# Down projection, first half: one matmul of 512 columns where there were two of 256

## The chip, the cores and the metric

The kernel runs on one core of one Trainium2 chip. The metric is the device time of one execution in microseconds, as a median of several runs. Beside the timed runs stands one profiled execution with its trace; all rows below come from that execution. Engines: PE is TensorE's matmul (PEld its weight load), DVE VectorE, ACT ScalarE, POOL GpSimd, SP the queue that issues the DMAs.

## The reference

One layer of a diffusion backbone runs over 128 context and 2048 latent tokens (2176 tokens in all, 1024 wide). What matters here is its last part, the feed-forward block and the final norm:

```python
h2 = rmsnorm(x, norm2) * (1 + scale2) + shift2
up = conv3(h2 @ w_up)                 # 1024 -> 2 * 2816, three taps
a, gg = jnp.split(up, 2, axis=-1)
x = x + gate2 * ((jax.nn.silu(gg) * a) @ w_down)   # 2816 -> 1024
y = rmsnorm(x, final_norm)
```

All data are float32. The mLSTM scans, the short convolution and the output projection before it are not touched.

## The kernel before

Features lie on the 128 partitions and tokens on the free axis, so that a matmul has a 128x128 block of a weight matrix as its stationary operand and a row of tokens as its moving one. To keep float32 precision each operand is split into a rounded high part and a remainder (`wh`, `wl` and `th`, `tl`), and each product is three matmuls: high by high, high by low, low by high.

The up and the down projection are both computed by a seven-product block scheme. Tokens are cut in two halves `hf` of `HN = (1024, 1152)`, each of two blocks `blk` (512 or 576 tokens). The down projection is 14 products `w` (`PRODS`, seven for each half). A product has four units `mp`, one for each pair of output rows. A unit runs over the 11 tiles of the contraction in three steps (`KS = (4, 4, 3)`), so there are 12 steps in a product. In a step, for each piece `p` of the unit's tokens, each tile issues the three matmuls of lines 1201 to 1203 into that piece's own PSUM bank, `acc[p]`. Before the change a unit's block of tokens is two pieces of a quarter of the half: 256 columns in the first half, 288 in the second. The banks come in the turn `abcabca` from a pool of seven (three named `pa`, two `pb`, two `pc`); an eighth, `st`, serves the norms.

Around the matmuls:

- Weights. `stages` loads one 704 KB block a unit into `st` (line 328, two buffers), and `part` makes `wh` on ACT (line 278) and `wl` on DVE (line 279), a step at a time, two steps ahead of the matmuls (three buffers each). The load of the next unit waits until DVE is done with the buffer.
- Tokens. `Chunk` loads one of three parts of the next product's moving operand (`F<-uD`, line 1042, two buffers) and splits it into `tH` and `tL` (lines 1048 and 1049) in a ring of six.
- Results. After a unit's last step `close` (line 1068) adds its bank, times the gate, to each of the one to four output blocks that this product belongs to (`DOWN`), on DVE: one instruction for a piece, two for the piece in which context ends and latent tokens begin. The seven products of a half have 14 such blocks, times four units.
- Norms. When a block of tokens is complete, its squares are summed (lines 1078 and 1079). `norm` then makes the reciprocal root, in `inv_rms` (PE column sums, line 128; DVE, line 131; POOL, line 132) and `spread` (PE, line 139), scales the eight output tiles (line 1091), stores them (`out_y<-o`, line 1095) and loads the second half's residual into the same buffers (`o<-xD`, line 1060). It is a generator, `fin`, and is advanced by one piece a step, or by two in the second half's products 0 and 5. In the first half it runs once for each of the two pieces: the first piece only scales, the second scales, stores and loads.

SP carries all of these transfers in one queue. Within a queue instructions run in the order that was set when the kernel was built. Independent work may stand there in another order than in the code, as the rows below show it.

Of the kernel before, what the change touches and what calls it, by code (L numbers as in the profile page):

```python
# [35 lines left out]
HN = (1024, 1152)  # L36
# [15 lines left out]
def spans(t0, t1):  # L52

    return [(a, b, v) for a, b, v in ((t0, min(t1, P), 0), (max(t0, P), t1, 1)) if a < b]
# [3 lines left out]
def hymba_kernel(ctx: ExitStack, tc: tile.TileContext, I, O):  # L58
    nc = tc.nc
    V, S, G, PE, Q = nc.vector, nc.scalar, nc.gpsimd, nc.tensor, nc.sync  # L60
# [61 lines left out]
    def inv_rms(ss, n, r):  # L122

        nch = (n + P - 1) // P
        ps = pst.tile([P, 512], F32, name="st")
        for i in range(nch):
            w = min(P, n - i * P)
            PE.matmul(ps[:w, i:i + 1], ss[:, i * P:i * P + w], ones[:, 0:1], start=True, stop=True)
        for i0, i1, w in ((0, n // P, P), (n // P, nch, n % P)):
            if i0 < i1 and w:  # L130
                V.tensor_scalar(r[:w, i0:i1], ps[:w, i0:i1], 1.0 / D, EPS, op0=ALU.mult, op1=ALU.add)
                G.tensor_tensor(r[:w, i0:i1], r[:w, i0:i1], mhalf[:w, i0:i1], op=ALU.pow)

    def spread(r, n):

        ps = pst.tile([P, 512], F32, name="st")
        for i in range((n + P - 1) // P):
            w = min(P, n - i * P)
            PE.matmul(ps[:, i * P:i * P + w], bc(r[:w, i:i + 1], [w, P]), ident[:w, :w], start=True, stop=True)
        return ps  # L140
# [14 lines left out]
    def squares(b, xt):  # L155
        n = BL[b][1]
        ss = ssp.tile([P, 384], F32, name="ss")
        for k in range(KT):
            x = xt[k // 4][:, k % 4, :n]
            if k == 0:  # L160
                S.activation(ss[:, :n], x, AF.Square)
                continue
            sq = sqp.tile([P, 384], F32, name="sq")
            S.activation(sq[:, :n], x, AF.Square)
            V.tensor_add(ss[:, :n], ss[:, :n], sq[:, :n])
        return ss
# [27 lines left out]
    def make_h(b, src, norm):  # L194
        return apply(b, load_x(b, src, xp, "xt", 2), norm)
# [122 lines left out]
                k: (lambda mp, i=i: wD[mp, i]) for i, k in enumerate(("s1", "s2", "s4", "s3"))}}  # L318
    PRODS = [(hf, x) for hf in range(2) for x in range(7)]

    def units_of(w):
        if w == 13:
            return [(mp, (p,)) for p in range(2) for mp in range(4)]
        return [(mp, (0, 1)) for mp in range(4)]
# [643 lines left out]
    with ph2:  # L968
# [5 lines left out]
        def bank(kind):  # L974
            return pu.tile([P, 512], F32, name="p" + kind, bufs=3 if kind == "a" else 2)
# [77 lines left out]
        outs, sst = {}, {}  # L1053

        def load_out(hf, m, blk):
            n = HN[hf] // 2
            t0 = hf * HN[0] + blk * n
            t = (op if blk else dp).tile([P, 576], F32, name=f"o{m}")
            outs[m, blk] = t[:, :n]
            Q.dma_start(outs[m, blk], xD[m][:, t0:t0 + n])  # L1060

        def close(hf, m, blk, p, acc):
            n = HN[hf] // 4
            t0 = hf * HN[0] + (2 * blk + p) * n
            q = outs[m, blk][:, p * n:(p + 1) * n]
            for a, e, v in spans(t0, t0 + n):
                a, e = a - t0, e - t0
                V.scalar_tensor_tensor(q[:, a:e], acc[:, a:e], modT[:, 40 + m, v:v + 1], q[:, a:e],
                                       op0=ALU.mult, op1=ALU.add)

        def square(m, blk, a, e, first=False):
            if first:
                if a == 0:
                    sst[blk] = dp.tile([P, 576], F32, name="ss", bufs=2)
                S.activation(sst[blk][:, a:e], outs[m, blk][:, a:e], AF.Square)
                return
            sq = dp.tile([P, 576], F32, name="sq", bufs=2)
            S.activation(sq[:, a:e], outs[m, blk][:, a:e], AF.Square)
            V.tensor_add(sst[blk][:, a:e], sst[blk][:, a:e], sq[:, a:e])

        def norm(hf, blk, p, then=None):

            n = HN[hf] // 4
            t0 = hf * HN[0] + 2 * blk * n
            r = dp.tile([P, 4], F32, name="fr", bufs=2)
            inv_rms(sst[blk][:, p * n:(p + 1) * n], n, r)
            yield
            rb = spread(r, n)
            for m in range(KT):
                q = outs[m, blk][:, p * n:(p + 1) * n]  # L1090
                V.scalar_tensor_tensor(q, q, nrm[:, 2, m:m + 1], rb[:, :n], op0=ALU.mult, op1=ALU.mult)
                if hf:
                    Q.dma_start(O["y"][m][:, t0 + p * n:t0 + (p + 1) * n], q)
                elif p:
                    Q.dma_start(O["y"][m][:, t0:t0 + 2 * n], outs[m, blk])
                    then(m)
                if m % 2:
                    yield
# [4 lines left out]
                yield  # L1103

        def norms(hf, blk):
            for p in range(2):
                yield from norm(hf, blk, p, lambda m: load_out(1, m, blk))

        split(0, ORDER[2])
# [6 lines left out]
        def take():  # L1116
            w = next(prods, None)
            if w:
                ahead.append(w)
            return ahead.pop(0)  # L1120

        for hf, j, i in ((hf, j, i) for hf in range(2) for j in range(FT) for i in range(7)):
# [13 lines left out]
            for p in range(2):  # L1136
# [3 lines left out]
                for kk in range(4):  # L1140
                    rh, rl = (t[:, 4 * p + kk] for t in slots[ORDER[i]])
                    w = slice(kk * P, (kk + 1) * P)
# [7 lines left out]
                m, blk, other = {3: (0, 1, 2), 4: (1, 1, 1), 5: (0, 0, 0), 6: (1, 0, None)}[i]  # L1150
# [35 lines left out]
        fin = iter(())  # L1186
        step = 0
        for w, (hf, x) in enumerate(PRODS):
            n = HN[hf] // 4
            for mp, ps in units_of(w):  # L1190
                acc = {p: bank(next(turn))[:, :n] for p in ps}
                for c, nk in enumerate(KS):
                    while loads and loads[0][0] - 3 <= step:
                        loads.pop(0)[1].load()
                    wh, wl = take()
                    th, tl = ds[RING[w % 2][c]]
                    for p in ps:
                        for kk in range(nk):
                            k = slice(kk * P, (kk + 1) * P)
                            t = slice((2 * kk + p) * n, (2 * kk + p + 1) * n)  # L1200
                            PE.matmul(acc[p], wh[:, k], th[:, t], start=(c == kk == 0), stop=False, skip_group_check=True)  # L1201
                            PE.matmul(acc[p], wh[:, k], tl[:, t], start=False, stop=False, skip_group_check=True)  # L1202
                            PE.matmul(acc[p], wl[:, k], th[:, t], start=False, stop=(c == 2 and kk == nk - 1),  # L1203
                                      skip_group_check=True)
                    if c == 2:
                        for row, blk in DOWN[x][2]:
                            for p in ps:
                                close(hf, mp + 4 * row, blk, p, acc[p])
                    if jobs and jobs[0][0] + 1 <= step:
                        k, ch = jobs[0]  # L1210
                        ch.split(step - k - 1, 2)
                        if step == k + 2:
                            jobs.pop(0)
                    if w == 0:
                        next(cv, None)
                    if step == 9:
                        for _ in cv:
                            pass
                        phu.close()
                        dp = ph2.enter_context(tc.tile_pool(name="dp", bufs=1, side="right"))  # L1220
                        for m in range(KT):
                            load_out(0, m, 0)
                    for _ in range(2 if hf and x in (0, 5) else 1):
                        next(fin, None)
                    step += 1
                if w == 13:
                    square(mp, 0, ps[0] * n, (ps[0] + 1) * n)
                    if ps == (0,) and mp == 3:
                        fin = norm(hf, 0, 0)
            if x == 4:  # L1230
                fin = chain(squares(hf, 1, range(KT), True), norms(hf, 1))
            if x == 5:
                fin = chain(fin, squares(hf, 0, range(4, KT), True))
            if w == 6:
                fin = chain(fin, squares(hf, 0, range(4), False), norms(hf, 0))
# [68 lines left out]
```

## Time and profile before

| | |
|---|---|
| median of 3 runs | 2519.47 us (2518.98 to 2521.13) |
| profiled execution | 2520.55 us, of which the span of its instructions is 2518.8 us |
| PE busy | 98% of the span |
| DVE, ACT, POOL busy | 69%, 44%, 3% |

The span is what the trace covers; the rest of the execution's time lies around it. Matmuls overlap one another, so that the duration of one says little; what counts is the distance from the start of one to the start of the next.

### The profile page before, as it was taken

To read this page: it belongs to the slowest core of one execution; us is meant where nothing else is said; L and a number is where in the kernel's file an instruction comes from. 1 tells how busy PE (TensorE), PEld (TensorE's weight loads), DVE (VectorE), ACT (ScalarE), POOL (GpSimd) and SP (SyncE) were. 2 spreads that over 40 slices of the span, in tenths; PEclk is the share of its full clock that TensorE was granted. 3 is DMA by queue.
4 is the path that set the end of the run, shared out by engine and by line. 5 is a ranking of instruction groups with operands and counts; after the bars stand their busy time and mean duration, and the time that the engine had idled before them with its cause. 6 is when DMAs were issued, how large, how long until landed. Compare 5 with 4: busy or idle time off the path is not lost.

```text
span 2518.8 us, 46131 instructions
## 1 busy us (share of the span) xinstructions
PE 2464.3 (98%) x17967; PEld 2446.1 (97%) x17967; DVE 1740.9 (69%) x3401; ACT 1100.6 (44%) x2109; POOL 67.0 (3%) x130
## 2 busy tenths in 40 slices
PE   8999999999999989999999999999999999999998
PEld 8999999999999989999999999999999999999998
DVE  4995443343467767889798879776767787677665
ACT  4521143333344444555454446544545543443343
POOL 0000000000011110000000000000000000000000
PEclk9999999999999999999999999999999999999999
DMA  8888733466567886977456446544444485576544
GB/s 287 281 278 268 224 102 105 140 205 211 175 199 205 256 272 199 291 249 250 149 198 210 151 158 229 186 155 157 149 163 143 158 299 202 189 241 221 181 158 145
DMA packets 252445, 506.29 MB, mean 201 GB/s; under 512 B 22963, under 2 KB 153155, under 8 KB 241347
## 3 DMA queue, kind: packets, MB, share of 16 engines
q1 hardware_dynamic: 252226, 503.35, 60.5%
q8 instruction: 141, 2.31, 0.4%
q14 instruction: 78, 0.63, 0.1%
HBM read 355.24 MB, written 148.03 MB: 200 GB/s over the span
## 4 chain that ended last, share of the span: by engine, by line
PE 77%; DVE 9%; DMA 9%; issue 2%; ACT 2%; SPq 1%; POOL 0%; DVEq 0%; ACTq 0%; POOLq 0%
PE pa L1143 7%; PE pa L1145 7%; PE pa L1144 7%; PE acc L206 5%; PE acc L208 5%; PE acc L207 5%; PE pb L1145 3%; PE pb L1143 3%; PE pb L1144 3%; DVE jk L555 3%; PE pa L1203 2%; PE pa L1201 2%; PE pa L1202 2%; DMA wD<-wm 2%; DMA R<-nD 2%; PE pc L1144 2%
## 5 line engine op out<-in xcount | busy, mean ns | idle before, releaser
L206 PE MATMUL acc<-hH,wh 128*128 128x384 f32 (+1 forms) x1536 | 513.7, 334 | 5.5 <-DVE cr L425 3.0
L208 PE MATMUL acc<-hH,wl 128*128 128x384 f32 (+1 forms) x1536 | 504.9, 329 | 0.0
L207 PE MATMUL acc<-hL,wh 128*128 128x384 f32 (+1 forms) x1536 | 504.2, 328 | 0.0
L1143 PE MATMUL pa<-tH,wh 128*128 128x272 f32 x1408 | 409.2, 291 | 4.1 <-DVE row L483 2.9
L1145 PE MATMUL pa<-tH,wl 128*128 128x272 f32 x1408 | 407.9, 290 | 0.0
L1144 PE MATMUL pa<-tL,wh 128*128 128x272 f32 x1408 | 405.9, 288 | 0.0
L278 ACT ACTIVATE wh<-st 128x512 fp32r<-128x512 f32 (+1 forms) x312 | 188.7, 609 | 418.9 <-PE pa L1144 118.2
L206 PEld LDWEIGHTS acc<-hH,wh 128*128 128x128 f32 x1536 | 290.3, 189 | 7.5 <-DVE cr L425 3.4
L207 PEld LDWEIGHTS acc<-hL,wh 128*128 128x128 f32 x1536 | 290.1, 189 | 0.7
L208 PEld LDWEIGHTS acc<-hH,wl 128*128 128x128 f32 x1536 | 290.1, 189 | 0.3 <-issue 0.2
L984 DVE SCALAR_TENSOR_TENSOR tt<-raw,fw,tt 128x127 f32<-128x127 f32 (+4 forms) x264 | 242.2, 947 | 47.3 <-ACT tt L990 46.2
L279 DVE TENSOR_TENSOR wl<-st,wh 128x512 fp32r<-128x512 f32 (+1 forms) x312 | 205.4, 660 | 98.8 <-ACT wh L278 93.3
L1143 PEld LDWEIGHTS pa<-tH,wh 128*128 128x128 f32 x1408 | 265.7, 189 | 5.1 <-DVE row L483 3.1
L1144 PEld LDWEIGHTS pa<-tL,wh 128*128 128x128 f32 x1408 | 266.1, 189 | 0.0
L1145 PEld LDWEIGHTS pa<-tH,wl 128*128 128x128 f32 x1408 | 265.4, 189 | 0.0
L1143 PE MATMUL pb<-tH,wh 128*128 128x272 f32 x704 | 203.6, 289 | 0.4 <-ACT wh L278 0.4
L1145 PE MATMUL pb<-tH,wl 128*128 128x272 f32 x704 | 203.6, 289 | 0.0
L1144 PE MATMUL pb<-tL,wh 128*128 128x272 f32 x704 | 202.7, 288 | 0.0
L278 ACT ACTIVATE wh<-s 128x512 fp32r<-128x512 f32 x176 | 110.9, 630 | 148.1 <-PE pc L1144 90.5
L1203 PE MATMUL pa<-tH,wl 128*128 128x256 f32 (+1 forms) x528 | 152.6, 289 | 0.2 <-DVE wl L279 0.2
L1201 PE MATMUL pa<-tH,wh 128*128 128x256 f32 (+1 forms) x528 | 152.8, 289 | 0.0
L1202 PE MATMUL pa<-tL,wh 128*128 128x256 f32 (+1 forms) x528 | 152.4, 289 | 0.0
(236 smaller groups left out, 5485.3 us busy)
## 6 DMA issues: line engine op xcount, KB each, us to landing
st<-in_w_up SPq DMA_DIRECT2D x88, 512.0 KB, 4.5
wst<-in_w_in SPq DMA_DIRECT2D x48, 512.0 KB, 4.2
wU<-s SPq DMA_DIRECT2D x22, 1024.0 KB, 6.6
s<-wU SPq DMA_DIRECT2D x22, 1024.0 KB, 5.7
st<-wD SPq DMA_DIRECT2D x32, 704.0 KB, 4.9
st<-in_w_down SPq DMA_DIRECT2D x28, 704.0 KB, 4.1
R<-nD SPq DMA_DIRECT2D x34, 512.0 KB, 5.6
wm<-in_w_modr SPq DMA_DIRECT2D x32, 512.0 KB, 4.9
```

Source lines behind the costliest of these rows:

```text
L206: PE.matmul(acc[:, :n], w_h, hH[:, k, :n], start=(k == 0), stop=False)
L207: PE.matmul(acc[:, :n], w_h, hL[:, k, :n], start=False, stop=False)
L208: PE.matmul(acc[:, :n], w_l, hH[:, k, :n], start=False, stop=(k == KT - 1))
L278: S.activation(wh[:, :n], a, AF.Copy)
L279: V.tensor_sub(wl[:, :n], a, wh[:, :n].bitcast(F32))
L984: V.scalar_tensor_tensor(o, i, w, o, op0=ALU.mult, op1=ALU.add)
L1143: PE.matmul(acc, wh[:, w], rh, start=(kk == 0 and i in (0, 1, 5)), stop=False, skip_group_check=True)
L1144: PE.matmul(acc, wh[:, w], rl, start=False, stop=False, skip_group_check=True)
L1145: mm = PE.matmul(acc, wl[:, w], rh, start=False, stop=(kk == 3), skip_group_check=True)
L1201: PE.matmul(acc[p], wh[:, k], th[:, t], start=(c == kk == 0), stop=False, skip_group_check=True)
L1202: PE.matmul(acc[p], wh[:, k], tl[:, t], start=False, stop=False, skip_group_check=True)
L1203: PE.matmul(acc[p], wl[:, k], th[:, t], start=False, stop=(c == 2 and kk == nk - 1), skip_group_check=True)
```

## The change

In the first half of the down projection a unit has one piece of 512 columns, a whole PSUM bank, where it had two of 256. `NP` gives the number of pieces in each half. `close`, `norm` and the slices of the moving operand follow it, so that in the first half the norm of a block runs once over 512 tokens. The second half stays as it was.

```diff
+    NP = (1, 2)
+
     def units_of(w):
+        if w < 7:
+            return [(mp, (0,)) for mp in range(4)]
         if w == 13:
...
         def close(hf, m, blk, p, acc):
-            n = HN[hf] // 4
-            t0 = hf * HN[0] + (2 * blk + p) * n
+            n = HN[hf] // 2 // NP[hf]
+            t0 = hf * HN[0] + (NP[hf] * blk + p) * n
...
         def norm(hf, blk, p, then=None):
-            n = HN[hf] // 4
-            t0 = hf * HN[0] + 2 * blk * n
+            n = HN[hf] // 2 // NP[hf]
+            t0 = hf * HN[0] + NP[hf] * blk * n
...
-                elif p:
-                    Q.dma_start(O["y"][m][:, t0:t0 + 2 * n], outs[m, blk])
+                else:
+                    Q.dma_start(O["y"][m][:, t0:t0 + n], q)
                     then(m)
...
         def norms(hf, blk):
-            for p in range(2):
+            for p in range(NP[hf]):
                 yield from norm(hf, blk, p, lambda m: load_out(1, m, blk))
...
         for w, (hf, x) in enumerate(PRODS):
-            n = HN[hf] // 4
+            n = HN[hf] // 2 // NP[hf]
...
-                            t = slice((2 * kk + p) * n, (2 * kk + p + 1) * n)
+                            t = slice((NP[hf] * kk + p) * n, (NP[hf] * kk + p + 1) * n)
```

## Rows read from the trace of the kernel before

**Rows 1.** The page's first lines: span, busy time and share of each engine, instructions.

```profile
span 2518.8 us, 46131 instructions
...
PE 2464.3 (98%) x17967; PEld 2446.1 (97%) x17967; DVE 1740.9 (69%) x3401; ACT 1100.6 (44%) x2109; POOL 67.0 (3%) x130
```

**Rows 2.** Busy time by stretch, first half of the down projection, in six stretches.

```profile
core 0: us, PE busy (x) PEld busy (x) DVE busy (x) ACT busy (x) POOL busy (x), PEclk, DMA share, GB/s
2024.00:2064.00 40.00, 40.00 (x337) 40.00 (x336) 33.06 (x51) 19.10 (x28) 0.00 (x0) 1.00 0.85 316
2064.00:2104.00 40.00, 40.00 (x336) 40.00 (x336) 36.64 (x76) 17.41 (x25) 0.00 (x0) 1.00 0.68 230
...
2224.00:2247.00 23.00, 23.00 (x192) 22.80 (x191) 17.00 (x31) 9.50 (x15) 0.00 (x0) 1.00 0.94 322
sum 223.00, PE 223.00 PEld 222.80 DVE 168.68 ACT 100.64 POOL 1.96; mean PE 37.17 PEld 37.13 DVE 28.11 ACT 16.77 POOL 0.33
```

**Rows 3.** What PE waited for in the whole span: us in total, times, longest.

```profile
PE pb L1201 <- ACT wh L278: 3.2, 1, 3.2
...
PE st L139 <- POOL fr L132: 2.9, 3, 1.1
...
PE pa L1203 <- DVE wl L279: 0.2, 1, 0.2
```

**Rows 4.** Groups by line and shape, PE: the first of the three lines of matmuls.

```profile
line engine op names shapes xcount | busy us, mean ns | idle before us <-releasers
...
L1201 PE MATMUL pa<-tH,wh 128*128 128x256 f32 x264 | 74.7, 283 | 0.0
...
L1201 PE MATMUL pb<-tH,wh 128*128 128x256 f32 x176 | 50.0, 284 | 0.0
...
L1201 PE MATMUL pc<-tH,wh 128*128 128x256 f32 x176 | 49.8, 283 | 0.0
```

**Rows 5.** PE in order of time: first and last of 103 matmuls of 256 columns.

```profile
start us, us, engine line op out<-in xcount [idle before <-releaser]
2101.80 0.28 PE L1203 MATMUL pc<-tH,wl 128*128 128x256 f32 x1
...
2113.97 0.28 PE L1203 MATMUL pb<-tH,wl 128*128 128x256 f32 x1
```

**Rows 6.** The same: first and last of 101 matmuls of 288 columns.

```profile
2317.71 0.30 PE L1202 MATMUL pb<-tL,wh 128*128 128x288 f32 x1
...
2330.94 0.30 PE L1203 MATMUL pa<-tH,wl 128*128 128x288 f32 x1
```

**Rows 7.** The same, output of w_in: first and last of 47 of 384 columns.

```profile
96.17 0.34 PE L206 MATMUL acc<-hH,wh 128*128 128x384 f32 x1
...
104.14 0.33 PE L207 MATMUL acc<-hL,wh 128*128 128x384 f32 x1
```

**Rows 8.** The same, another 47 of 384 columns.

```profile
176.92 0.34 PE L206 MATMUL acc<-hH,wh 128*128 128x384 f32 x1
...
185.01 0.34 PE L207 MATMUL acc<-hL,wh 128*128 128x384 f32 x1
```

**Rows 9.** Groups by line and shape, DVE, 2024 to 2247 us.

```profile
L1068 DVE SCALAR_TENSOR_TENSOR o<-pa,modT,o 128x256 f32<-128x256 f32 x36 | 16.4, 477 | 1.3 <-PE pa L1203 1.3
...
L1091 DVE SCALAR_TENSOR_TENSOR o<-o,nrm,st 128x256 f32<-128x256 f32 x16 | 6.9, 474 | 0.0
...
L1068 DVE SCALAR_TENSOR_TENSOR o<-pa,modT,o 128x128 f32<-128x128 f32 x20 | 6.0, 342 | 3.4 <-PE pa L1203 3.4
```

**Rows 10.** In order of time, DVE and then PE: start of product 1's second unit.

```profile
2061.98 1.29 DVE L279 TENSOR_TENSOR wl<-st,wh 128x512 fp32r<-128x512 f32 x2 [1.91 <-ACT wh L278]
...
2063.11 0.28 PE L1201 MATMUL pa<-tH,wh 128*128 128x256 f32 x1
```

**Rows 11.** SP in order of time, second half's first product (time is that of issuing).

```profile
2257.53 0.32 SPq L328 DMA_DIRECT2D st<-wD  x1
2264.69 0.32 SPq L1042 DMA_DIRECT2D F<-uD  x1
2268.96 2.30 SPq L1095 DMA_DIRECT2D out_y<-o  x4
2271.60 2.68 SPq L1060 DMA_DIRECT2D o<-xD  x4
2274.33 2.27 SPq L1095 DMA_DIRECT2D out_y<-o  x4
2278.21 2.21 SPq L1060 DMA_DIRECT2D o<-xD  x4
2280.47 0.90 SPq L328 DMA_DIRECT2D st<-in_w_down  x2
```

**Rows 12.** PE in order of time, 2284.7 to 2291.4 us.

```profile
2284.76 0.29 PE L1203 MATMUL pa<-tH,wl 128*128 128x288 f32 x1
2288.24 0.61 PE L1201 MATMUL pb<-tH,wh 128*128 128x288 f32 x1 [3.19 <-ACT wh L278]
...
2291.29 0.36 PE L1202 MATMUL pb<-tL,wh 128*128 128x288 f32 x1
```

**Rows 13.** Busy time in the stretch behind that wait (columns as in rows 2).

```profile
2288.70:2291.00 2.30, 2.30 (x11) 2.30 (x11) 1.29 (x3) 0.43 (x2) 0.00 (x0) 0.50 0.57 203
```

## The prediction

> **What bounds the kernel now.** I read the page's first lines before anything else. PE is busy for 98% of the span, DVE for 69%, ACT for 44% [rows 1]. A sum over stages can mislead, so I cut the first half of the down projection into stretches. There PE is busy in all of the 223 us, at the full granted clock of 1.00 (2.4 GHz). DVE is busy for 168.68 us of them, but for 36.64 of 40 us between 2064 and 2104, and the DMA engines are 94% busy in the last 23 us [rows 2]. The list of PE's waits confirms it: in the down projection's loop it stood once, 3.2 us, for weights, three times for POOL in the norms, 2.9 us together, and 0.2 us for a remainder of weights [rows 3]; all but the last of these lie behind the 223 us. So in the changed stage the distance from one matmul to the next sets the time, and anything else counts only if it makes PE wait.
>
> **The matmuls.** The rows of line 1201 sum to 264 + 176 + 176 = 616 matmuls of 256 columns, and the three lines make 1848 of them [rows 4]. Afterwards there are 924 of 512 columns. The same columns are streamed; 924 matmuls and 924 weight loads go.
>
> What one costs is read from starts, because durations overlap. With 256 columns 103 starts span 2113.97 - 2101.80 = 12.17 us, 119.3 ns each [rows 5]. With 288 it is 13.23 us over 100 distances, 132.3 ns [rows 6]. With 384 there are two cases: 7.97 us over 46, 173.3 ns [rows 7], and 8.09 us over 46, 175.9 ns [rows 8]. A column at 2.4 GHz takes 0.417 ns, so 256 columns take 106.7 ns, 288 take 120.0 and 384 take 160.0. What is left for each matmul is 12.6, 12.3, and 13.3 to 15.9 ns. It hardly grows with the columns: it is a price for a matmul, and half of the matmuls no longer pay it.
>
> No row shows 512 columns. The kindest extrapolation takes the slope between 256 and 288 (13.0 ns over 32 columns, 0.406 ns a column): 119.3 + 256 x 0.406 = 223.3 ns. The harshest takes the slope from 288 to the slow 384 (43.6 ns over 96, 0.454): 175.9 + 128 x 0.454 = 234.0 ns. A pair of 256 costs 2 x 119.3 = 238.6 ns, so a pair gains 4.6 to 15.3 ns, and 924 pairs 4.3 to 14.1 us. Between them lie 213.3 ns of columns plus the 384's own 13.3 to 15.9, which is 226.6 to 229.2. I take 228 ns, since 384 is the nearest row: 10.6 ns a pair, **9.8 us** in all.
>
> The Trainium skill speaks against so much: its page "TensorE: Matmul & The Clock Gate", section "Wait — 56ns, not 53.3ns?", gives a warm matmul its columns at 2.4 GHz and only about 2.5 ns beside them. By that rule 924 matmuls fewer would gain an estimated 2.3 us. This case's rows don't agree for these float32 pairs of weight load and matmul: 256 columns would take 109.2 ns by the rule and take 119.3.
>
> **DVE.** A close of 256 columns is 477 ns in the mean and one of 128 columns 342 ns [rows 9], 1.05 ns a column. One of 512 is then 477 + 256 x 1.05 = 746 ns, against 954 for two. By the time in which they were busy (16.4 us for 36 and 6.0 us for 20) the pair is 911 ns and the one 767. With 14 blocks times four units there are 56 pairs, so DVE is relieved of 8 to 12 us. The piece with the context tokens stays cut at 128. The norms' scaling loses 16 of 32 instructions in the same way. This buys nothing directly, since PE doesn't wait for DVE here. It does matter that PE will ask for its weights 5% faster: DVE's 168.68 us in 223 become some 158 in 213, the same 75%.
>
> A bank of 512 columns is complete only at the unit's end, where before the first piece was complete nine matmuls (1.1 us) earlier. So the closes start that much later, and end at about the same time, being shorter. With one bank a unit instead of two, a bank is asked for again after seven units instead of three and a half, which is the cover: I cost this at nothing. Without it the price would be one close, 0.75 us, at each of 28 units.
>
> **Norm.** Column sums and spreading work on 128 tokens at a time, so PE has the same number of them. DVE's and POOL's steps run once instead of twice a block. The eight stores and eight loads of a block stay, but their order changes: they come with the first, now only, pass, five advances of `fin` earlier. That is five steps (13 us at 223 / 84 = 2.65 us a step) for the block finished in the first half, and two and a half steps for the one finished behind it, where two advances are made a step. On SP they will pass other weight and token loads than before, and this is the part that no row of before can settle.
>
> The price is in the rows. In the second half's first product, SP issued a weight load at 2257.53, a token load at 2264.69, then 16 stores and loads until 2280.4, and only then two weight loads at once [rows 11]. The first of these was late: PE stood for 3.19 us until ACT had made its `wh`, and started again at half clock, 0.50 [rows 12, 13]. From 2284.76 to 2291.29 there are 13 starts; at 132.3 ns they would have taken 1.7 us and took 6.5. So this wait cost 4.8 us. Moved to an earlier place, the 16 transfers may leave that load free (a gain of up to 4.8 us), or delay another one as much (a loss of about as much if the old wait stays too). I take 0 with both ends kept. The wait for POOL, 1.1 us at most [rows 3], stays: there the column sums and the spreading are still one advance apart.
>
> **Sum.** 2520.55 us of the profiled execution - 9.8 = 2510.7 us. That execution lies 1.1 us above the median of 2519.47, so I forecast 2519.47 - 9.8 = 2509.7 us, 0.39% less. A difference of 0.2%, 5 us, is about what a measurement can tell from none.
>
> **Rivals.**
>
> *The late weight load disappears.* The stores no longer stand ahead of the load at 2280.47. For it speaks that they move forward by more than two steps; against it, that the other loads of that product had only the same queue. Gain 9.8 + 4.8 = 14.6 us: 2504.9 us.
>
> *The supply doesn't follow.* Where DVE and DMA are busiest, weights arrive shortly before they are needed: in product 1's second unit the first of two remainders that end at 2063.27 was done at about 2062.6, and PE began at 2063.11 [rows 10], half a microsecond later. PE gains 66/2 x 10.6 = 0.35 us a unit, so by that sixth unit it would come 1.7 us earlier, and stand for about 1.2 us unless DVE's shorter closes make up for it. Together with a second delayed load of 3 to 4 us half of the gain is lost: about 2514.5 us.
>
> *The 12 to 16 ns aren't the matmul's own price*, but come with the columns (a slower stream from SBUF, say). For it speaks that the remainder is largest at 384; against it, that it is no larger at 288 than at 256. At 119.3 / 256 = 0.466 ns a column 512 take 238.6 ns, as much as the pair, and nothing is gained; but 384 would then take 178.9 ns, and even the slow case is 175.9. At 175.9 / 384 = 0.458 ns 512 take 234.5 ns and 3.8 us are gained. So 2515.7 to 2519.5 us, no change that a measurement can tell. By the rule of the Trainium skill's page named above the result would be an estimated 2517 us.
>
> *Slower*, by one mechanism: the 16 transfers, now earlier, hold up weight loads on SP in both places. Each stop costs 4.8 us, so it takes more than two such new stops to eat 9.8 us, and more than three (9.8 + 5.0 = 14.8 us) to be slower by over 0.2%. For it speaks that 94% of the DMA engines' time was taken where the first block's transfers ended [rows 2]; against it, that these now come before that stretch. Four stops would give about 2529 us.
>
> **Chances.** The forecast with small changes of the waits (2506 to 2514) 0.57; the late load gone 0.20; supply or a new wait 0.12, half of it still over 0.2% faster; no price of the matmul's own 0.07; slower 0.04. That makes faster 0.57 + 0.20 + 0.06 = 0.83, same 0.06 + 0.07 = 0.13, slower 0.04. For 8 in 10 I take 2503.5 to 2514 us: the forecast, the better case, and the nearer edge of the supply case; the bounds of a pair alone give 2505.4 to 2515.2.
>
> **What would show it.** Right: 924 matmuls of 512 columns, starts 226 to 230 ns apart, a first half of the down projection of some 213 us, closes of 512 columns near 750 ns, DVE's share unchanged. Wrong: starts above 234 ns, an idle PE behind line 278 or 279 in products 0, 1 or 6, or a stop of more than 3 us behind a weight load that SP issued after a row of stores.

## The result, and the profile after

The changed kernel takes 2506.47 us in the median of six runs (2500.30 to 2509.24), beside 2520.30 us for the kernel before on the same chip. The ratio is 0.9939 with a 95% interval of 0.9925 to 0.9952: 0.61% faster, 12 to 19 us (the medians alone differ by 13.8 us). The forecast was faster by 9.8 us, at 2509.7 us. The way was right, and so was the gain in the first half; a second gain came in the second half, where the forecast had put 0. The profiled execution took 2504.05 us.

The page's first lines, after:

```profile
span 2502.2 us, 44204 instructions
...
PE 2454.3 (98%) x17043; PEld 2398.2 (96%) x17043; DVE 1731.5 (69%) x3327; ACT 1100.3 (44%) x2109; POOL 62.9 (3%) x128
```

Against [rows 1] 924 matmuls are gone and the span is 16.6 us shorter. To see where, both traces are divided at the down projection's matmuls: at the start of the first, of the first of the second half and of the last. The kernel before has these at 2023.66, 2246.92 and 2506.51 us, the changed one at 2023.90, 2237.48 and 2490.66 us. So the first half lasts 213.6 us in place of 223.3 (9.7 less), the second half, which the change doesn't touch, 253.2 in place of 259.6 (6.4 less), and what lies behind the last start 0.7 less.

The changed matmuls, in order of time: first and last of 54 in a row, and the groups of their first line by shape.

```profile
2101.82 0.40 PE L1207 MATMUL pa<-tL,wh 128*128 128x512 f32 x1
...
2113.94 0.39 PE L1206 MATMUL pb<-tH,wh 128*128 128x512 f32 x1
```

```profile
L1206 PE MATMUL pa<-tH,wh 128*128 128x512 f32 x132 | 51.5, 390 | 0.0
L1206 PE MATMUL pc<-tH,wh 128*128 128x512 f32 x88 | 34.7, 394 | 0.1
L1206 PE MATMUL pb<-tH,wh 128*128 128x512 f32 x88 | 34.4, 390 | 0.0
```

That is 12.12 us over 53 distances, 228.7 ns, against 119.3 ns for half as many columns [rows 5]. Over the whole stage the mean distance is 228.3 ns, and before it was 119.7, if the 10 of 923 and 11 of 1847 distances are left out in which PE stopped or worked for the norms; with all of them it is 231.1 and 120.8.

Busy time by stretch in the first half (columns as in [rows 2]):

```profile
2024.00:2064.00 40.00, 40.00 (x176) 32.51 (x175) 32.85 (x43) 19.93 (x29) 0.00 (x0) 1.00 0.89 326
...
2214.00:2237.00 23.00, 22.90 (x99) 18.14 (x98) 16.32 (x25) 11.71 (x17) 0.00 (x0) 1.00 0.91 337
sum 213.00, PE 212.90 PEld 174.50 DVE 159.90 ACT 102.37 POOL 1.20; mean PE 35.48 PEld 29.08 DVE 26.65 ACT 17.06 POOL 0.20
```

PE still has no room. DVE is busy for 159.90 of 213 us, the same three quarters as in [rows 2]; weight loads no longer fill PEld.

What PE waited for from 2015 to 2500 us, all of it:

```profile
PE st L139 <- POOL fr L132: 1.9, 2, 1.1
PE st L128 <- DVE ss L1084: 1.7, 1, 1.7
```

The wait of 3.2 us for weights [rows 3] is gone, and one of the three for POOL, of 1.0 us. The wait of 1.7 us for DVE, behind the last of these matmuls, was there before with the same length. The reason why the weights are in time stands in SP's queue in the second half's first product, the answer to [rows 11]:

```profile
2247.91 0.32 SPq L333 DMA_DIRECT2D st<-wD  x1
2250.78 2.57 SPq L1100 DMA_DIRECT2D out_y<-o  x4
2255.63 2.12 SPq L1065 DMA_DIRECT2D o<-xD  x4
2257.80 2.69 SPq L1100 DMA_DIRECT2D out_y<-o  x4
2263.13 2.84 SPq L1065 DMA_DIRECT2D o<-xD  x4
2266.02 1.78 SPq L333 DMA_DIRECT2D st<-in_w_down  x2
```

The 16 transfers still stand ahead of the weight load for product 8's first unit. That load is now issued 28.5 us after the second half began (2266.02 - 2237.48), where it was 33.6 us (2280.47 - 2246.92). The next two rows show how little more than enough that is in this execution: DVE finishes the first remainder of these weights at 2273.53 + 0.69 = 2274.22, and PE begins the product at 2274.58.

```profile
2273.53 0.69 DVE L279 TENSOR_TENSOR wl<-st,wh 128x512 fp32r<-128x512 f32 x1 [1.28 <-ACT wh L278]
...
2274.58 0.29 PE L1206 MATMUL pb<-tH,wh 128*128 128x288 f32 x1
```

### The profile page after: what moved, and what is told of

The parts are those of the page before. It is cut to its first block, busy times and chain, and to the rows that moved or that the text cites. A ratio compares the mean times of both kernels' runs of the same rounds, so it can differ in the third digit from the quotient of the medians.

```text
span 2502.2 us, 44204 instructions
## 1 busy us (share of the span) xinstructions
PE 2454.3 (98%) x17043; PEld 2398.2 (96%) x17043; DVE 1731.5 (69%) x3327; ACT 1100.3 (44%) x2109; POOL 62.9 (3%) x128
## 4 chain that ended last, share of the span: by engine, by line
PE 79%; DMA 8%; DVE 8%; issue 1%; ACT 1%; SPq 1%; POOL 0%; DVEq 0%; ACTq 0%; POOLq 0%
PE pa L1148 7%; PE pa L1150 7%; PE pa L1149 7%; PE acc L206 6%; PE acc L208 6%; PE acc L207 6%; PE pb L1150 4%; PE pb L1148 3%; PE pb L1149 3%; DVE jk L560 3%; PE pa L1206 3%; PE pa L1207 3%; PE pa L1208 3%; DMA wD<-wm 2%; PE pc L1208 2%; PE pc L1206 2%
## 5 line engine op out<-in xcount | busy, mean ns | idle before, releaser
L114 DVE TENSOR_TENSOR wl<-wst,wh 128x512 fp32r<-128x512 f32 (+1 forms) x160 | 105.9, 687 | 64.2 <-ACT wh L111 64.2
L279 DVE TENSOR_TENSOR wl<-s,wh 128x512 fp32r<-128x512 f32 x176 | 120.7, 687 | 29.0 <-ACT wh L278 25.4
L1148 PEld LDWEIGHTS pb<-tH,wh 128*128 128x128 f32 x704 | 132.4, 188 | 0.6 <-ACT wh L278 0.6
```

Of the source, the lines that this page charges most:

```text
L114: V.tensor_sub(wl[:, a:a + n // 2], st[:, a:a + n // 2], wh[:, a:a + n // 2].bitcast(F32))
L279: V.tensor_sub(wl[:, :n], a, wh[:, :n].bitcast(F32))
L1148: PE.matmul(acc, wh[:, w], rh, start=(kk == 0 and i in (0, 1, 5)), stop=False, skip_group_check=True)
```

## The experiments

In the comparisons below the runs of one kernel lie up to 18 us apart, and in the profiles the down projection starts anywhere from 2017.2 to 2030.9 us, by what happens before it. So beside each ratio to the kernel before stand the two halves of the down projection from the one profile of each kernel, each from the start of its first matmul to the start of its last. For the kernel before they are 223.1 and 259.6 us, for the changed one 213.4 and 253.2.

**The matmuls alone.** Units, banks and closes as in the changed kernel, the first half's norms in two passes again.

```diff
         def norm(hf, blk, p, then=None):
-            n = HN[hf] // 2 // NP[hf]
-            t0 = hf * HN[0] + NP[hf] * blk * n
+            n = HN[hf] // 4
+            t0 = hf * HN[0] + 2 * blk * n
...
-                else:
-                    Q.dma_start(O["y"][m][:, t0:t0 + n], q)
+                elif p:
+                    Q.dma_start(O["y"][m][:, t0:t0 + 2 * n], outs[m, blk])
...
-            for p in range(NP[hf]):
+            for p in range(2):
```

> Matmuls of 512 columns, one bank and one close as in the changed kernel, but the first half's norms again in two passes of 256 tokens, stores with the second pass. Theory (two separate gains: the price of 924 matmuls, and the single pass of the norm which moves 16 stores and loads ahead of a weight load): the first half of the down projection takes 213 to 214 us, and in the second half PE stands again for 2 to 5 us at the first unit of product 8, behind a weight load that was issued after the stores. Total 9 to 11 us below the kernel before, 4 to 7 us above the changed kernel. Rival (the earlier PE alone moved the queue, the norm edit does nothing): no such stand, and the time of the changed kernel within 2 us.

Ratio 0.9960 (0.9948 to 0.9973), halves of 217.9 and 259.6 us. The starts are 228.3 ns apart, stops again left out. PE's waits from 2015 to 2500 us, the longest sums among them:

```profile
PE pa L1206 <- ACT wh L278: 2.6, 2, 2.3
PE pb L1206 <- ACT wh L278: 2.3, 1, 2.3
PE st L139 <- POOL fr L132: 1.8, 2, 0.9
```

The second half keeps its stand, and all of its old length. The total is as expected, but not the first half: it lost 4.5 of its 9.7 us to new stands and a granted clock of 0.50 behind the largest of them. That one is of 2.3 us, until 2227.66 us, and in SP's queue a weight load left at 2220.20 us behind ten of the first block's 16 transfers: 7.5 us lie between, and in [rows 11, 12] it is 7.8 us from the late load to PE's start. That is the rival in which the supply doesn't follow, and only the other part of the edit keeps it away. Without the norm's single pass the 924 matmuls fewer are worth 5.2 us in this stage, about half.

**The norm alone.** The other half of the edit: units of two times 256 columns, the first half's norms in one pass of 512 tokens. The lines are given against the changed kernel.

```diff
     def units_of(w):
-        if w < 7:
-            return [(mp, (0,)) for mp in range(4)]
...
         def close(hf, m, blk, p, acc):
-            n = HN[hf] // 2 // NP[hf]
-            t0 = hf * HN[0] + (NP[hf] * blk + p) * n
+            n = HN[hf] // 4
+            t0 = hf * HN[0] + (2 * blk + p) * n
...
-                            t = slice((NP[hf] * kk + p) * n, (NP[hf] * kk + p + 1) * n)
+                            t = slice((2 * kk + p) * n, (2 * kk + p + 1) * n)
```

> Matmuls of 256 columns in two banks and closes of 256 as before the change; only the first half's norms run in one pass of 512 tokens. Theory of two separate gains: the first half of the down projection stays at 223 us, the stand of 3.2 us at product 8 and its half clock go, 4 to 7 us below the kernel before. Rival (the queue moved only because PE was earlier): within 2 us of the kernel before, with the stand of 3 us still there.

Ratio 0.9967 (0.9956 to 0.9978), halves of 224.0 and 254.2 us. The stand is gone, as expected by the theory of two gains; the ratio says 8 us, the halves 4.5. The rival, that the earlier PE alone moved the queue, falls with both runs: with an earlier PE and the old norm the stand is there, with the old PE and the new norm it isn't. The first half, 224.0 us, gains nothing by the norm.

**One bank, two matmuls.** Bank, close and norm of the changed kernel, but 256 columns a matmul.

```diff
-                    for p in ps:
+                    for p in ((0, 1) if hf == 0 else ps):
...
+                            m = HN[hf] // 4
+                            t = slice((2 * kk + p) * m, (2 * kk + p + 1) * m)
+                            o = acc[p] if hf else acc[0][:, p * m:(p + 1) * m]
...
```

> The changed kernel with its one bank, its closes of 512 columns and its norm in one pass, but each matmul of 512 columns issued as two of 256 into the two halves of that bank, in the order of the kernel before. Theory (a price for each matmul of 12 to 13 ns): 1848 matmuls 119 to 120 ns apart, the first half of the down projection 223 us, 9 to 11 us above the changed kernel. Rival (the gain came from fewer closes and from banks that come free earlier): 213 to 215 us for that stage, the time of the changed kernel within 2 us.

Ratio 0.9966 (0.9952 to 0.9979), halves of 225.6 and 253.2 us: the time of the run with the norm alone. By the ratios it is 7 us above the changed kernel, by the halves 12, of which 1.8 are short waits for weights. First and last of 103 matmuls in its first half:

```profile
2109.73 0.28 PE L1210 MATMUL pa<-tL,wh 128*128 128x256 f32 x1
...
2121.91 0.28 PE L1210 MATMUL pb<-tL,wh 128*128 128x256 f32 x1
```

12.18 us over 102 distances are 119.4 ns. So fewer closes and fewer banks gain nothing; the number of matmuls does. Each matmul here comes with a weight load of its own, and no run tells which of the two the price belongs to.

**The norm five advances later.**

```diff
         def norms(hf, blk):
+            for _ in range(5):
+                yield
             for p in range(NP[hf]):
```

> The changed kernel, but the generator of the first half's norms waits five advances before each norm, so that the single pass with its stores and loads comes where the second pass came before. If the place of the 16 stores and loads in the queue is what made the weight load late, PE stands again for 2 to 5 us in the second half's first two products: 4 to 7 us above the changed kernel. If it is the second pass itself (its scaling, its POOL step), nothing comes back: within 2 us of the changed kernel.

Ratio 0.9953 (0.9938 to 0.9967), halves of 216.6 and 259.9 us: 10 us above the changed kernel by the halves, and 3.5 by ratios whose intervals overlap. One pass, at the place of the old second pass, brings the stand back, and a smaller one in the first half:

```profile
PE pb L1208 <- ACT wh L278: 4.5, 1, 4.5
PE pa L1208 <- ACT wh L278: 1.9, 1, 1.9
```

So it is the place of the pass with its transfers, not the number of passes. Which of the two, the pass or SP's queue, the next run tells.

**Other queues and another order.** The 32 transfers of the first half's norms are issued by POOL, first in the kernel before and then in the changed one (the diff is that of the changed one).

```diff
-        def load_out(hf, m, blk):
+        def load_out(hf, m, blk, q=Q):
...
-            Q.dma_start(outs[m, blk], xD[m][:, t0:t0 + n])
+            q.dma_start(outs[m, blk], xD[m][:, t0:t0 + n])
...
-                    Q.dma_start(O["y"][m][:, t0:t0 + n], q)
+                    G.dma_start(O["y"][m][:, t0:t0 + n], q)
...
-                yield from norm(hf, blk, p, lambda m: load_out(1, m, blk))
+                yield from norm(hf, blk, p, lambda m: load_out(1, m, blk, G))
```

> The kernel before, with only the stores and the residual loads of the first half's norms issued from POOL's queue in place of SP's. If the weight load was late because it stood behind these 16 transfers in SP's queue, PE's stand of 3.2 us and its half clock go, the second half of the down projection takes 253 to 255 us in place of 259.6, the first half stays at 223 us: 4 to 7 us below the kernel before. If it was late because the transfers take the DMA engines' time wherever they are issued, the stand stays and the time is within 2 us of the kernel before.

Ratio 0.9982 (0.9970 to 0.9994), halves of 222.8 and 254.8 us. The same bytes move at nearly the same time, but no longer ahead of the weights. SP's and POOL's rows around it:

```profile
2265.03 7.96 SPq L328 DMA_DIRECT2D st<-in_w_down  x2
```

```profile
2263.76 2.41 POOL L1095 DMA_DIRECT2D out_y<-o  x4 [2.79 <-DVE o L1091]
...
2272.36 2.42 POOL L1095 DMA_DIRECT2D out_y<-o  x4
```

The load is issued 23.8 us after the second half began (at 2241.24), in the midst of the stores, and PE doesn't stand for it. SP's queue was the cause, not the DMA engines' time. The total gained 4.5 us by the ratio, at the low end of what was expected (the medians differ by 6.6 us).

> The changed kernel once more, on the chip of the next three. The down projection's two halves should take 213 to 215 us and 253 to 255 us again. If the weight load for product 8's first unit, which was ready only 0.4 us before its use in the first profile, is a matter of luck, the second half may take up to 258 us here.

The changed kernel once more on that chip: ratio 0.9938 (0.9918 to 0.9957), halves of 213.3 and 253.2 us, the load at 27.4 us.

> The changed kernel with the same 32 transfers on POOL's queue. If SP's queue is all that is left of that effect, PE stands nowhere in products 5 to 8, halves of 212 to 214 us and 252 to 254 us: equal to the changed kernel or up to 3 us below it. If POOL's queue costs something of its own, slower than the changed kernel by 1 us or more.

The changed kernel with POOL's queue: ratio 0.9933 (0.9914 to 0.9951), halves of 213.3 and 253.3 us, the load at 21.7 us. That load's first remainder is done 3.0 us before PE begins product 8, where it was 0.4 us in the first profile of the changed kernel and 1.5 us in the second; the time is the same.

> The changed kernel with the eight residual loads behind the eight stores of a block, and not in between. SP then waits once and not several times for stores to land, so the block of transfers gets shorter: the weight load for product 8 is issued 2 to 4 us earlier against PE than in the changed kernel, no stand in products 5 to 8, time equal to the changed kernel or up to 3 us below. If the planner puts the loads elsewhere and delays another weight load, 2 to 5 us above it.

This edit had a slip: it issued the residual loads behind the second half's norms too, over tiles that are still in use there, so its time isn't that of the idea (ratio 0.9953, 0.9935 to 0.9970; halves of 213.4 and 259.5 us). It shows the same mechanism at another place: in SP's queue a weight load leaves at 2453.41 us behind 16 such transfers, and PE stands for 2.9 us until 2461.19 us for `wh`. The next run mends it.

```diff
                     Q.dma_start(O["y"][m][:, t0:t0 + n], q)
-                    then(m)
                 if m % 2:
                     yield
+            if then and not hf:
+                for m in range(KT):
+                    then(m)
+                    if m % 2:
+                        yield
```

> The changed kernel with the eight residual loads of the first half's norms behind the eight stores of a block, and not in between; the second half's norms stay as they were. One wait of SP for landing stores instead of several: halves of 213 to 214 us and 252 to 254 us, no stand in products 5 to 8; equal to the changed kernel or up to 2 us below. If the planner lets the loads delay another weight load, 2 to 5 us above it.

Ratio 0.9921 (0.9903 to 0.9938), a median of 2502.61 us over four runs, halves of 212.9 and 253.2 us. Its queue:

```profile
2250.41 5.55 SPq L1100 DMA_DIRECT2D out_y<-o  x8
2256.01 3.79 SPq L1065 DMA_DIRECT2D o<-xD  x8
2259.90 7.54 SPq L333 DMA_DIRECT2D st<-in_w_down  x2
```

From 2195 to 2270 us SP stands in the changed kernel 12.5 us, in eleven waits, until stores have landed:

```profile
SPq L1065 <- DMA out_y<-o: 12.5, 11, 4.1
```

In this run the same stretch has no such wait at all, where one was expected, and the weight load leaves 22.8 us after the second half began (at 2237.11). This is the lowest median of all (the run over widths, further down, leaves columns out), but its interval overlaps that of the changed kernel: it isn't told apart from it. Nor is the room at the tightest load much larger, though the load leaves 5.7 us earlier: its first remainder is done at 2272.48 us and PE begins at 2274.21, 1.7 us later, where the changed kernel's two profiles have 0.4 and 1.5 us.

Put together, the load's place separates the long second halves from the short ones:

| kernel | load after the half's start, us | second half, us |
|---|---|---|
| before | 33.6 | 259.6 |
| matmuls alone | 33.5 | 259.6 |
| norm late | 33.2 | 259.9 |
| changed | 28.5 | 253.2 |
| one bank, two matmuls | 28.0 | 253.2 |
| norm alone | 27.8 | 254.2 |
| before, POOL's queue | 23.8 | 254.8 |
| changed, loads last | 22.8 | 253.2 |

Where the load leaves 33 us or more behind the start, the half lasts 6 us longer; among those that leave by 28.5 us an earlier one buys nothing. The 1.0 and 1.6 us by which the norm alone and POOL's queue lie above 253.2 are in products 7 and 13, at other and shorter stops.

**What a matmul costs beside its columns.** Two runs read only the upper 16 bits of each operand word in the first half, which is every second half-word (the diff is the same in the kernel before and in the changed one), and one varies the columns.

```diff
+                            b = (lambda x, s: x[:, s] if hf else x[:, s].bitcast(mybir.dt.bfloat16)[:, 1::2])
-                            PE.matmul(acc[p], wh[:, k], th[:, t], start=(c == kk == 0), stop=False, skip_group_check=True)
+                            PE.matmul(acc[p], b(wh, k), b(th, t), start=(c == kk == 0), stop=False, skip_group_check=True)
...
```

> The kernel before, but the first half's 1848 matmuls read only the upper 16 bits of each word of their two operands (bfloat16, every second half-word), so that the first half's products lose precision; columns, order and everything else stay. If the 12 to 13 ns beside the columns belong to float32 operands, starts come nearer to 256 / 2.4 = 106.7 ns, 107 to 113 ns, and the stage takes 200 to 210 us unless the weights arrive too late. If they belong to any matmul with its weight load, starts stay at 119 to 120 ns.

```profile
2101.82 0.27 PE L1204 MATMUL pb<-tH,wl 128*128 128x256 bf16 x1
...
2113.95 0.27 PE L1203 MATMUL pa<-tL,wh 128*128 128x256 bf16 x1
```

> The changed kernel with the same 16-bit operands in the first half's 924 matmuls of 512 columns. Price of float32: starts 214 to 218 ns apart. Price of any matmul: 226 to 229 ns as in the changed kernel. Together with the run of 256 columns it tells what two of 256 cost over one of 512 without float32: 2 to 10 ns in the first case, 11 ns in the second.

```profile
2101.61 0.39 PE L1208 MATMUL pa<-tL,wh 128*128 128x512 bf16 x1
...
2113.79 0.39 PE L1208 MATMUL pb<-tL,wh 128*128 128x512 bf16 x1
```

With 256 columns there are 108 starts, 113.4 ns apart; with 512 there are 55, 225.6 ns apart. The expectation for a price of float32 was just missed at 256 columns (107 to 113 ns) and clearly at 512 (214 to 218 ns); that for a price of any matmul missed at 256 (119 to 120 ns) and nearly held at 512 (226 to 229 ns). The halves are 214.4 and 262.8 us with 256 columns, where the second half's load leaves 37 us behind the start, and 211.9 and 254.4 us with 512, where it leaves after 29 us. With 256 the first half was expected at 200 to 210 us unless weights come too late, and PE waited 1.8 us for weights there. With 16-bit operands two matmuls of 256 (226.8 ns) cost as much as one of 512, to within 1.2 ns.

```diff
+                            N = n if hf or c == kk == 0 else (512, 448, 384, 320, 256, 192, 128)[w]
+                            t = slice(t.start, t.start + N)
-                            PE.matmul(acc[p], wh[:, k], th[:, t], start=(c == kk == 0), stop=False, skip_group_check=True)
+                            PE.matmul(acc[p][:, :N], wh[:, k], th[:, t], start=(c == kk == 0), stop=False, skip_group_check=True)
...
```

> The changed kernel, but product w of the first half streams only 512, 448, 384, 320, 256, 192 and 128 columns (w = 0 to 6) in all but the first three matmuls of each unit, so that the other columns of its sums stay incomplete; only the distance of the starts within a product is read. A price of 13 ns beside the columns at 2.4 GHz, whatever their number: 226, 200, 173, 146, 120, 93 and 66 ns. A rate of 0.443 ns a column, as the 16-bit matmuls of 256 and 512 columns have it: 227, 198, 170, 142, 113, 85 and 57 ns. A floor from the float32 weight load, as the 129-column matmuls elsewhere show it: not below 110 to 112 ns at 192 and 128 columns.

Starts of 29 float32 matmuls in one unit of products 1 to 5, first and last (28 distances):

```profile
2061.90 0.36 PE L1208 MATMUL pb<-tH,wh 128*128 128x448 f32 x1
...
2067.57 0.36 PE L1209 MATMUL pb<-tL,wh 128*128 128x448 f32 x1
...
2095.89 0.34 PE L1208 MATMUL pc<-tH,wh 128*128 128x384 f32 x1
...
2100.76 0.33 PE L1209 MATMUL pc<-tL,wh 128*128 128x384 f32 x1
...
2118.75 0.30 PE L1208 MATMUL pa<-tH,wh 128*128 128x320 f32 x1
...
2122.85 0.31 PE L1209 MATMUL pa<-tL,wh 128*128 128x320 f32 x1
...
2138.78 0.27 PE L1208 MATMUL pa<-tH,wh 128*128 128x256 f32 x1
...
2142.12 0.28 PE L1209 MATMUL pa<-tL,wh 128*128 128x256 f32 x1
...
2153.37 0.26 PE L1208 MATMUL pa<-tH,wh 128*128 128x192 f32 x1
...
2156.47 0.28 PE L1209 MATMUL pa<-tL,wh 128*128 128x192 f32 x1
```

These are 202.5, 173.9, 146.4, 119.3 and 110.7 ns. Less the columns at 2.4 GHz (186.7, 160.0, 133.3, 106.7, 80.0) there remain 15.8, 13.9, 13.1, 12.6 and 30.7 ns, and 15.0 ns for the 512 of the changed kernel. From 256 columns up it is the near-constant price that the forecast took. At 192 the distance is 8.6 ns less than at 256, where the columns alone would make it 26.7 less: it lies where the third expectation put a floor. Product 6, with 128 columns, was short of weights and ran at a granted clock of 0.50, and isn't read.

## Why the prediction was right, and where it was too small

*The bound.* PE's distances set the stage: 924 matmuls fewer took 9.7 us from it, where 9.8 were forecast, and 213.4 us remained of the "some 213". The price for a matmul was taken as 228 ns for 512 columns, and the mean is 228.3. By the two means a pair gained 11.1 ns, which is 10.3 us; some 0.6 us of it went into the distances left out of them, so that the agreement to 0.1 us is partly chance. The rival by which the remainder comes with the columns falls for float32: it put 512 columns at 234.5 to 238.6 ns, and by the run over widths its 0.466 ns a column would make 448 columns 208.8 ns, and they took 202.5. One reading of the prediction was wrong, and changed no term: the wait of 0.2 us [rows 3], which it set inside the 223 us, stands in the last product.

```profile
2502.40 0.41 PE L1203 MATMUL pa<-tH,wl 128*128 128x288 f32 x1 [0.20 <-DVE wl L279]
```

*DVE.* A close of 512 columns was forecast at 746 ns:

```profile
L1073 DVE SCALAR_TENSOR_TENSOR o<-pa,modT,o 128x512 f32<-128x512 f32 x13 | 9.5, 744 | 1.8 <-PE pa L1208 1.8
```

DVE was to be busy for some 158 of 213 us, and was for 159.9. That this buys nothing by itself is shown by the run with one bank and two matmuls.

*Norm.* This is the step whose size was off: "I take 0 with both ends kept". It was worth 6.4 us in the second half: the stand and its half clock, 4.8 us by [rows 12, 13], and about 1 us where the norm's second pass and its wait for POOL are gone; the last product, in which that wait of 0.2 us stood, lasts 36.9 us in place of 37.5. The run of the norm alone has 5.4 us of it. The late load's rival, put at 2504.9 us with a chance of 0.20, was the case that came: 2519.5 x 0.9939 is 2504.1. Mechanism and price were on record. The time alone would not have told: the median of 2506.47 us also lies at the lower edge of the forecast's own 2506 to 2514, and it is the profile that shows the load on time. What the rows of before couldn't give was how much earlier the load would go: it was 5.1 us, and that was enough with 0.4 us of room in one profile and 1.5 us in the other. That it sufficed was not forecast, and so far it is luck. The run with the late norm and the one with POOL's queue show that this place in SP's queue moves the time.

*The supply.* The forecast gave it 1.2 us in products 0 and 1 and a second delayed load. In the changed kernel neither shows as idle time of PE. The runs of the matmuls alone and of the late norm show that it was near: 2.3 and 1.9 us of standing at the end of the first half, in product 6, as soon as the transfers stood in their old place.

*Slower.* The mechanism, transfers that hold up weight loads in both places, exists: with the transfers in their old place it cost 3.2 us (late norm) and 4.5 us (matmuls alone) of the first half's gain, on top of the second half's old loss. That is far from the 14.8 us that it needed.

## What to carry to other kernels

Where PE has no idle time, count matmuls and not only columns: with float32 operands each, with its weight load, cost 12 to 16 ns beside its columns, so that filling a bank with one matmul in place of two gained 11 ns a pair here; with 16-bit operands, read as they were here, a pair would have gained about 1 ns. Look at what else the edit reorders: some 40% of this gain (6.4 of 16.1 us in the two halves) came with stores and loads that wait for other work, and that now stand elsewhere in the one queue that also feeds the weights. Where such transfers make a load late that PE needs, give them to an idle queue, which gained 4.5 us in the kernel before, or issue the stores together and the loads that wait on them behind. Once the load is in time, as in the changed kernel, neither is shown to gain more.

## What the runs showed of the hardware

Float32 matmuls with a weight load each started 110.7 ns apart at 192 columns; those of 129 columns in line 870 of the kernel before start 111 to 112 ns apart as well, so that this looks like a floor. From 256 columns up the distance is the columns at 2.4 GHz plus 12.3 to 15.9 ns in the rows shown here. With 16-bit operands, every second half-word, it is 0.443 ns a column at 256 and 0.441 at 512, 6% above 2.4 GHz at a granted clock of 1.00, and a pair of 256 costs only 1.2 ns more than one of 512. Why the one has a constant part and the other a rate isn't settled by these runs. The weight loads differ as well: their median durations are 188 ns in the changed kernel and 96 ns in the run of 512 columns with 16-bit operands:

```profile
L1206 PEld LDWEIGHTS pb<-tH,wh x264: 187/188/191, 2031.3 to 2481.5; 128*128 128x128 f32 x132
```

```profile
L1207 PEld LDWEIGHTS <-wh x308: 96/96/181, 2026.6 to 2237.8; 128*128 128x128 bf16 x154
```

As 188 ns is longer than the 110.7 ns between two starts, such a duration isn't the price of a load.

The Trainium skill, "TensorE: Matmul & The Clock Gate", section "Wait — 56ns, not 53.3ns?", gives back-to-back matmuls at 2.4 GHz about 2.5 ns beside their columns, which is an estimated 109.2 and 215.8 ns for 256 and 512. Neither the float32 nor the 16-bit rows of this case, in which every matmul has its own weight load, agree with it: 119.3 and 228.7 ns, 113.4 and 225.6 ns.
